# Key norms and values by one-pass transposes, sums and centring on VectorE, and a new order of the planned region

## The chip, the cores and the metric

The kernel runs on one core of a Trainium2 chip. Its five engines work side by side: TensorE (PE in the profile; PEld is its weight loads), VectorE (DVE), ScalarE (ACT), GpSimd (POOL) and SyncE (SP, which here only issues DMAs). The metric is the time of one execution in microseconds of the device. Three runs of the kernel before took 892.96, 894.33 and 895.68 us, so the median is 894.33 us. One further execution was profiled; it took 893.92 us, and its trace spans 891.5 us from the first instruction to the last.

## The reference, cut to what matters

One decoder layer on 16 meta tokens and 512 tokens of width 1024, in float32: a sliding-window attention and an RWKV-7 time mixing with 16 heads of 64, merged by gates, then an output projection, a layer norm and an MLP. The change touches the time mixing alone:

```python
kk = kh * k_k.astype(f32).reshape(H, N)
kk = kk / jnp.maximum(jnp.sqrt(jnp.sum(kk * kk, -1, keepdims=True)), 1e-12)
...
def step(S, inp):
    r_t, w_t, k_t, v_t, kk_t, a_t = inp
    sa = jnp.einsum('bhij,bhj->bhi', S, -kk_t)
    S = S * w_t[:, :, None, :] + sa[..., None] * (kk_t * a_t)[:, :, None, :] + v_t[..., None] * k_t[:, :, None, :]
    return S, jnp.einsum('bhij,bhj->bhi', S, r_t)
...
ym = jnp.mean(y, -1, keepdims=True)
yv = jnp.mean(jnp.square(y - ym), -1, keepdims=True)
y = ((y - ym) * lax.rsqrt(yv + GN_EPS)).reshape(B, T, W) * lnx_g.astype(f32) + lnx_b.astype(f32)
```

For each head and token this needs the sum of 64 squared keys (the key norm), and it takes the mean of 64 outputs away from each output before the variance. The output is linear in v, so a v whose mean over the 64 channels of a head has been taken away gives outputs whose mean is already away.

## The kernel before, in words

The program has two parts. The first, up to about 560 us of the trace, is a region planned by hand: the functions `lead`, `head`, `rwkv`, `attention`, `merge`, `merged`, `out_half` and `first_norm` do not emit instructions but record 3087 operations, each with an engine, the buffers that it reads and writes, and a closure that emits it. `Plan.order` then emits them in the order of the list `ORDER`; `SLOTS` says for each new buffer which slot of its ring it gets (eight PSUM banks in the ring `rg`, and rings in SBUF). Each engine takes its instructions in that order, and waits where an input or a slot is not free yet. The second part, the MLP, is written in order behind the region and is not touched.

The time mixing and the attention work on pairs of heads: `rwkv(j)` and `attention(j)` for j from 0 to 7, with 128 channels (two heads of 64) on the partitions and 528 tokens along the row. Dense products (`dense`, eight input blocks of 128, two at a time) split every float32 weight and input in two parts of a shorter float type and take three products (lines 454 to 456 of the profile); ACT makes the one part of the weights (line 611) and DVE the other (line 613). They stand between the many small steps of the pairs in the order, and are what PE does while a pair waits.

A product of plain float32 operands stands in the trace as two records, a transpose (`pe.transpose`, a product with the identity) as one. The steps that the change touches are, in each pair:

- **Key norms**, `norms`, lines 987 to 989. `sq` holds the squared scaled keys, channels on partitions. Five float32 products with `ones2`, a constant of two columns that has a one where a channel belongs to a head, give the two sums per token, tokens on partitions, in ten columns of the bank `mt`. A sixth product for the meta tokens (line 989) goes to the same bank. DVE clamps the ten columns (line 992) and takes the reciprocal (line 994), and POOL spreads the result to `dv`, `dvm` and `dvx` (lines 999 to 1008), by which scores are scaled (line 1039) on the way to the triangular solve of the pair, a long row of small steps on POOL (lines 1122 and 1126).
- **Values**, `turn_v`, line 1096, and `meta0`, lines 1194 and 1195. Four float32 products of v with `center` (the identity less 1/64 within a head) turn v to tokens on partitions and centre it at the same time; a fifth does so for the meta tokens.
- **The state and the outputs**. `link` (line 1243) carries the state from one chunk of 64 tokens to the next, with a scaling on DVE (line 1225) and on ACT (line 1228) between two links; `outs` (line 1253) gives the outputs in the bank `Y`.
- **Group norm of the outputs**, lines 1264 to 1277: ACT squares `Y` into `ysq`, DVE sums each 64 (line 1265) and scales the sums (line 1266), POOL takes the power -1/2 (line 1267), DVE multiplies `Y` by it into `yn` (line 1268), PE turns it back by transposes (`turn_y`, line 1273), ACT applies gain and bias (line 1276) and POOL adds the bonus (line 1277). The last pair does this in two halves, since the output projection (lines 1418 to 1420) and the first norm (line 1482 and on) wait for it.

Of the kernel before, what the change touches and what calls it, by code (L numbers as in the profile page):

```python
# [14 lines left out]
AF = mybir.ActivationFunctionType  # L15
# [61 lines left out]
for _name, _c in ROWS:  # L77
# [304 lines left out]
def hybrid_layer_kernel(ctx: ExitStack, tc: tile.TileContext, I: dict, out: bass.AP):  # L382
# [26 lines left out]
    def cv(name):  # L409
        a, w = CONSTS[name]  # L410
        return con[:, a : a + w]
# [1621 lines left out]
```

## Time and profile before

| | |
|---|---|
| runs | 892.96, 894.33, 895.68 us; median 894.33 us |
| the profiled execution's own time | 893.92 us |
| its span | 891.5 us, granted TensorE clock 0.996 |
| ACT busy | 518.1 us (58%) |
| POOL busy | 286.3 us (32%) |
| DMA | 115.85 MB, mean 130 GB/s |

A line of a busy table gives the busy time of an engine and its share of the span, then the number of its instructions. In the line by slices each digit is the busy share, in tenths, of a fortieth of the span (22.3 us). A group of instructions reads: line, engine, operation, what it writes and reads with shapes, the count, busy time in us, mean duration in ns, and the idle time of the engine just ahead of it with what ended it. A line of a timeline reads: start in us, duration in us, engine, line, operation. The duration of a product on PE is from its start until its last result is out, and the next one starts long before that; what a product takes of PE's time is the distance from its start to the next start. ACT and DVE also do the splitting of the weights for PE, and POOL the triangular solves; the DMA queues load weights all through the span.

### The profile page before, as it was taken

The page shows a single profiled execution, that of the slowest core. Times are in us where ns is not written, and L with a number is a line of the kernel's source. Part 1 is how long each engine was busy: PE and PEld are TensorE (multiplying, and loading weights), DVE is VectorE, ACT ScalarE, POOL GpSimd, SP SyncE. Part 2 cuts the span into 40 slices and gives each one's busy share as a digit, 9 for nine tenths or more (in the row PEclk, how much of TensorE's full clock was granted, in tenths as well). Part 3 has the DMA queues.
Part 4 walks back from the last instruction along what each step waited for, and adds up shares of the span by engine and source line. Part 5 has one row for each costly group of instructions (what it writes and reads, how often), then busy time and mean ns, then how long its engine had stood idle before and what let it go on. Part 6 is the DMA issues. An engine that isn't in the chain of part 4 may idle for free.

```text
span 891.5 us, 17504 instructions
## 1 busy us (share of the span) xinstructions
PE 873.5 (98%) x6712; PEld 764.2 (86%) x6712; DVE 675.8 (76%) x1192; ACT 518.1 (58%) x1131; POOL 286.3 (32%) x672
## 2 busy tenths in 40 slices
PE   7999999999999999999999999999999999999996
PEld 7899989898898988887878777988888888888885
DVE  7665876878778678568588789597877886788757
ACT  8645658546585584563855545755555655564700
POOL 4038265275472751832836602000010000000001
PEclk9999999999999999999999999999999999999999
DMA  7233324322524323232345631485687578576222
GB/s 267 88 102 106 101 90 112 83 67 57 153 72 113 123 67 94 67 101 62 117 104 167 193 107 53 123 280 147 165 214 205 149 209 245 142 201 165 99 92 94
DMA packets 73531, 115.85 MB, mean 130 GB/s; under 512 B 40310, under 2 KB 47736, under 8 KB 69480
## 3 DMA queue, kind: packets, MB, share of 16 engines
q1 hardware_dynamic: 69728, 98.89, 35.6%
q0 software_dynamic: 2880, 14.68, 9.1%
q8 instruction: 52, 0.85, 0.4%
q10 hardware_dynamic: 840, 1.17, 0.4%
q14 instruction: 31, 0.25, 0.1%
HBM read 107.56 MB, written 8.21 MB: 130 GB/s over the span
## 4 chain that ended last, share of the span: by engine, by line
PE 80%; POOL 6%; DVE 6%; issue 4%; ACT 2%; DMA 1%; SPq 0%; DVEq 0%; POOLq 0%; ACTq 0%
PE g L454 9%; PE g L455 9%; PE g L456 9%; PE dnR L1798 7%; PE rq L1704 5%; PE tp L1704 4%; PE dnP L1798 4%; PE last L1798 4%; PE dnT L1798 3%; PE up L455 3%; PE up L454 3%; PE up L456 3%; POOL Xf L1126 2%; POOL ftmp L1122 2%; PE g L1182 2%
## 5 line engine op out<-in xcount | busy, mean ns | idle before, releaser
L454 PE MATMUL g<-hhi,whi 128*128 128x512 f32 (+3 forms) x640 | 211.9, 331 | 0.4 <-ACT whi L611 0.4
L455 PE MATMUL g<-hlo,whi 128*128 128x512 f32 (+3 forms) x640 | 203.6, 318 | 0.1
L456 PE MATMUL g<-hhi,wlo 128*128 128x512 f32 (+3 forms) x640 | 203.4, 318 | 0.2 <-DVE wlo L613 0.2
L454 PEld LDWEIGHTS g<-hhi,whi 128*128 128x128 f32 x640 | 120.8, 189 | 11.3 <-issue 1.4
L1122 POOL TENSOR_TENSOR ftmp<-Xf,Nf 108x84 f32<-108x84 f32 (+23 forms) x248 | 95.9, 387 | 104.2 <-DMA Nf<-Nd 75.3
L456 PEld LDWEIGHTS g<-hhi,wlo 128*128 128x128 f32 x640 | 120.6, 188 | 9.1 <-DVE wlo L613 0.8
L455 PEld LDWEIGHTS g<-hlo,whi 128*128 128x128 f32 x640 | 120.9, 189 | 7.6 <-DVE hlo L817 0.3
L613 DVE TENSOR_TENSOR wlo<-wraw,whi 128x512 fp32r<-128x512 f32 x126 | 89.7, 723 | 27.3 <-ACT whi L611 20.6
L1126 POOL TENSOR_TENSOR Xf<-Xf,ftmp 108x84 f32<-108x84 f32 (+23 forms) x248 | 104.2, 420 | 18.4
L611 ACT CAST whi<-wraw 128x512 fp32r<-128x512 f32 x126 | 76.6, 619 | 33.7 <-DMA wraw<-in_w_in_dram 15.9
L1788 POOL DMA_DIRECT2D braw<-in_w_ff_dram x12 | 10.7, 890 | 204.4 <-DVE wlo L1605 87.8
L1228 ACT ACTIVATE Z<-g,PC 64x64 f32<-64x64 f32 x64 | 19.7, 309 | 77.5 <-DVE Z L1225 39.9
L1605 DVE TENSOR_TENSOR wlo<-wraw,whi 128x1024 fp32r<-128x1024 f32 x22 | 26.9, 1222 | 12.8 <-ACT whi L1601 12.8
L1225 DVE TENSOR_SCALAR Z<-g,PC 64x64 f32<-64x64 f32 x64 | 17.5, 274 | 25.0 <-PE g L1243 11.9
L1267 POOL TENSOR_TENSOR rs<-rs,mhalf 128x8 f32<-128x8 f32 (+1 forms) x9 | 15.9, 1764 | 60.9 <-DVE rs L1266 60.8
L1601 ACT CAST whi<-wraw 128x1024 fp32r<-128x1024 f32 x22 | 22.9, 1042 | 18.2 <-PE dnR L1798 5.8
L1605 DVE TENSOR_TENSOR blo<-braw,bhi 128x1024 fp32r<-128x1024 f32 x25 | 30.5, 1219 | 2.4 <-ACT bhi L1601 2.4
L1605 DVE TENSOR_TENSOR wlo<-braw,whi 128x1024 fp32r<-128x1024 f32 x25 | 30.5, 1219 | 2.4 <-ACT whi L1601 2.4
L1601 ACT CAST whi<-braw 128x1024 fp32r<-128x1024 f32 x25 | 26.3, 1052 | 5.1 <-PE rq L1704 4.3
L1601 ACT CAST bhi<-braw 128x1024 fp32r<-128x1024 f32 x25 | 26.3, 1051 | 3.5 <-DMA braw<-in_w_ff_dram 3.5
L454 PE MATMUL up<-h1hi,whi 128*128 128x512 f32 x72 | 28.1, 390 | 0.0
L455 PE MATMUL up<-h1lo,whi 128*128 128x512 f32 x72 | 28.1, 390 | 0.0
(532 smaller groups left out, 2455.1 us busy)
## 6 DMA issues: line engine op xcount, KB each, us to landing
wraw<-in_w_in_dram SPq DMA_DIRECT2D x52, 512.0 KB
braw<-in_w_ff_dram SPq DMA_DIRECT2D x19, 1024.0 KB
wraw<-in_w_ff_dram SPq DMA_DIRECT2D x32, 512.0 KB
braw<-in_w_ff_dram POOLq DMA_DIRECT2D x12, 1024.0 KB, 8.3
wraw<-in_w_out_dram SPq DMA_DIRECT2D x14, 256.0 KB
Nf<-Nd SPq DMA_DIRECT2D x24, 144.0 KB
res<-in_x_dram SPq DMA_DIRECT2D x4, 512.0 KB
G<-in_consts_dram SPq DMA_DIRECT2D x16, 128.0 KB
```

The costliest lines, as they stand in the source:

```text
L454: pe.matmul(ps, whi, xhi, start=first, stop=False)
L455: pe.matmul(ps, whi, xlo, start=False, stop=False)
L456: pe.matmul(ps, wlo, xhi, start=False, stop=last)
L611: AC(512, lambda hi=hi, qs=qs: act.copy(hi.t, raw.t[:, qs]), plain=True, r=[raw], w=[hi], new=[hi])
L613: f = lambda hi=hi, lo=lo, qs=qs, e=e: e.tensor_tensor(lo.t, raw.t[:, qs], hi.t.bitcast(F32), op=ALU.subtract)
L1122: sub(nj * nt, lambda s=s, nj=nj, nt=nt, tv=tv: pool.tensor_tensor(tv(), Xf.t[:, 0:nj, s : s + 1].to_broadcast([NB, nj, nt]), Nf.t[:, s : ...
L1126: sub(nj * nt, lambda s=s, nj=nj, tv=tv: pool.tensor_tensor(Xf.t[:, 0:nj, s + 1 :], Xf.t[:, 0:nj, s + 1 :], tv(), op=ALU.add), port=1, r=[ ...
L1228: op("ACT", 335, lambda: act.activation(Z.t[H2[1], c, 1, :], src(1), AF.Copy, scale=PC.t[H2[1], last : last + 1]), r=[ps, PC], w=[(Z, ("s" ...
L1601: act.copy(like(s["r"][0][:, :n], s["x"]), s["x"])
L1605: dve.tensor_tensor(lo, s["x"], hi.bitcast(F32), op=ALU.subtract)
L1704: pe.matmul(o, l[:, ks], r[:, k], start=start and k == c == 0, stop=stop and k == 3 and c == 2, skip_group_check=True)
L1798: pe.matmul(acc[b], l[:, as_], r[:, ws], start=first and i == 0 and q == 0, stop=last and i == NP - 1 and q == 2, skip_group_check=True)
```

## The change

Three products become transposes, and VectorE does what the constants did. The operation counts of the other engines stay.

- `norms`: five transposes of `sq`, four into a bank of its own, `kt_`, and one into columns 128 to 255 of `mt`, and the product for the meta tokens as before. DVE sums each 64 of the four (one `tensor_reduce` over 512 columns) and then, in one operation `inverse`, each 64 of the meta tokens' 128 columns, the clamp and the reciprocal.
- `turn_v` and the second product of `meta0`: transposes with the identity, so v is not centred any more.
- The outputs: DVE sums each 64 of `Y` into the new `ym` and writes `yn` = `Y` - `ym`/64 (a `scalar_tensor_tensor`), ACT squares `yn` in place of `Y`, and the last multiplication works on `yn` in place.
- The constants `center` and `ones2` are gone, 130 columns of the table of constants.
- `ORDER` has 3105 operations (two more for each of nine output parts) and is another order throughout; `SLOTS` is written anew with it. The costs in the code say what the planner counts with: 1300 becomes 760 for `norms`, 896 becomes 442 for `turn_v`, 335 becomes 225 for `meta0`.

```diff
-    out["center"] = np.eye(P) - bones / HD
-    out["ones2"] = (p[:, None] // HD) == np.arange(2)[None, :]
...
+    rym = ring("ym", rb, [P, 8], 2)
...
-        mt, d1, dv, dvm = Buf(rg), Buf(rd1), new("dv", rdv), Buf(rdvm)
+        mt, kt_, d1, dv, dvm = Buf(rg), Buf(rg), Buf(rd1), new("dv", rdv), Buf(rdvm)
...
-                pe.matmul(mt.t[:, 2 * i : 2 * i + 2], sq.t[:, t0 : t0 + P], cv("ones2"), start=True, stop=True)
-            pe.matmul(mt.t[:, 8:10], sq.t[:, 0:P], cv("ones2"), start=True, stop=True)
+                pe.transpose(kt_.t[:, i * P : (i + 1) * P], sq.t[:, t0 : t0 + P], ident)
+            pe.transpose(mt.t[:, P : 2 * P], sq.t[:, 0:P], ident)
...
-        op("PE", 1300, norms, r=[sq, BKm, AXm], w=[(mt, "s")], new=[mt], mode="F")
-        op("DVE", 80, lambda: dve.tensor_scalar(d1.t, mt.t[:, 0:10], 1e-24, None, op0=ALU.max), r=[(mt, "s")], w=[d1], new=[d1])
-        op("DVE", 120, lambda: dve.reciprocal(d1.t, d1.t), r=[d1], w=[d1])
+        op("PE", 760, norms, r=[sq, BKm, AXm], w=[(mt, "s"), kt_], new=[mt, kt_], mode="F")
+        DV(512, lambda: dve.tensor_reduce(d1.t[:, 0:8], kt_.t.rearrange("p (u i) -> p u i", i=HD), axis=AX.X, op=ALU.add), r=[kt_], w=[d1], new=[d1])
+        def inverse():
+            dve.tensor_reduce(d1.t[:, 8:10], mt.t[:, P : 2 * P].rearrange("p (u i) -> p u i", i=HD), axis=AX.X, op=ALU.add)
+            dve.tensor_scalar(d1.t, d1.t, 1e-24, None, op0=ALU.max)
+            dve.reciprocal(d1.t, d1.t)
+        op("DVE", 400, inverse, r=[(mt, "s"), d1], w=[d1])
...
-                pe.matmul(vt.t[:, i * P : (i + 1) * P], v.t[:, t0 : t0 + P], cv("center"), start=True, stop=True)
-        op("PE", 896, turn_v, r=[v], w=[vt], new=[vt, Z], mode="F")
+                pe.transpose(vt.t[:, i * P : (i + 1) * P], v.t[:, t0 : t0 + P], ident)
+        op("PE", 442, turn_v, r=[v], w=[vt], new=[vt, Z], mode="T")
...
-            pe.matmul(ms.t[:, 0:P], v.t[:, 0:P], cv("center"), start=True, stop=True)
+            pe.transpose(ms.t[:, 0:P], v.t[:, 0:P], ident)
...
-            AC(n, lambda cs=cs: act.activation(ysq.t[:, cs], Y.t[:, cs], AF.Square), r=[(Y, k) for k in yk(j, h)], w=[(ysq, h)], new=[ysq] if one else [])
+            DV(n, lambda us=us, u8=u8: dve.tensor_reduce(ym.t[:, us], u8(Y.t), axis=AX.X, op=ALU.add), r=[(Y, k) for k in yk(j, h)], w=[(ym, h)], new=[ym] if one else [])
+            DV(n, lambda us=us, u8=u8: dve.scalar_tensor_tensor(u8(yn.t), B64(ym.t[:, us], HD), -1.0 / HD, u8(Y.t), op0=ALU.mult, op1=ALU.add),
+               r=[(ym, h)] + [(Y, k) for k in yk(j, h)], w=[(yn, h)], new=[yn] if one else [])
+            AC(n, lambda cs=cs: act.activation(ysq.t[:, cs], yn.t[:, cs], AF.Square), r=[(yn, h)], w=[(ysq, h)], new=[ysq] if one else [])
...
-            DV(n, lambda us=us, u8=u8: dve.tensor_tensor(u8(yn.t), u8(Y.t), B64(rs.t[:, us], HD), op=ALU.mult),
-               r=[(rs, h)] + [(Y, k) for k in yk(j, h)], w=[(yn, h)], new=[yn] if one else [])
+            DV(n, lambda us=us, u8=u8: dve.tensor_tensor(u8(yn.t), u8(yn.t), B64(rs.t[:, us], HD), op=ALU.mult),
+               port=1, r=[(rs, h)], w=[(yn, h)])
```

The rest of the diff is the two lists, `ORDER` and `SLOTS`.

More of the change, by code (lines that the diff above doesn't have):

```diff
@@ L1194, in meta0 @@
             pe.transpose(ms.t[0:48, 320:448], BKm.t, ident)
-            pe.matmul(ms.t[:, 0:P], v.t[:, 0:P], cv("center"), start=True, stop=True)
-        op("PE", 335, meta0, r=[BKm, v, XTm, AKm], w=[(ms, 0), (ms, "b")], new=[ms, BTm, SVm, RHm], mode="F")
+            pe.transpose(ms.t[:, 0:P], v.t[:, 0:P], ident)
+        op("PE", 225, meta0, r=[BKm, v, XTm, AKm], w=[(ms, 0), (ms, "b")], new=[ms, BTm, SVm, RHm], mode="F")
         DV(128, lambda: dve.tensor_tensor(BTm.t, ms.t[0:48, 320:448].rearrange("p (h j) -> p h j", h=2), B64(dvm.t, HD), op=ALU.mult),
@@ L1257, in rwkv @@
                w=[(Y, h)], new=[Y] if h == 0 else [], mode="C")
-        ysq, yn, rs = Buf(re_), Buf(re_), Buf(rrs)
+        ysq, yn, rs, ym = Buf(re_), Buf(re_), Buf(rrs), Buf(rym)
         yt, z = Buf(rg), new("z", rz)
```

323 rows, old and new, of tables (ORDER, SLOTS) are left out of this document.

## The prediction

> **What bounds the kernel now.** I read the page first, for which engine has no room, then the waits of PE, then busy time by stretch, and last the timeline of PE at the steps that change.
>
> ```profile
> span 891.5 us, 17504 instructions
> ...
> PE 873.5 (98%) x6712; PEld 764.2 (86%) x6712; DVE 675.8 (76%) x1192; ACT 518.1 (58%) x1131; POOL 286.3 (32%) x672
> ```
>
> PE is idle for 18.0 us of 891.5. The waits of PE, by what ended them, are 13 rows that sum to 9.6 us; the first three and the last:
>
> ```profile
> PE g L688 <- DMA con<-in_consts_dram: 3.2, 1, 3.2
> PE g L799 <- DVE res L766: 1.5, 1, 1.5
> PE g L1243 <- ACT Z L1228: 1.2, 3, 0.7
> ...
> PE g L456 <- DVE wlo L613: 0.2, 1, 0.2
> ```
>
> The first two belong to the start, ahead of any pair; no other row is over 1.2 us. So the planned region is a stream of products, and what PE no longer has to issue there shortens it, unless something else comes late in its place. How much room the other engines have shows in busy time by stretch (columns: stretch, its length, then PE, PEld, DVE, ACT, POOL, the granted clock, DMA share, GB/s): the whole region, and two stretches in which DVE is fullest.
>
> ```profile
> 0.00:560.00 560.00, 549.80 (x4918) 480.95 (x4919) 422.12 (x881) 342.79 (x878) 263.66 (x647) 1.00 0.37 106
> 320.00:360.00 40.00, 40.00 (x428) 34.95 (x428) 34.57 (x72) 23.43 (x58) 9.90 (x22) 1.00 0.29 76
> 520.00:560.00 40.00, 39.05 (x314) 31.18 (x314) 36.54 (x76) 22.75 (x56) 6.41 (x7) 1.00 0.22 67
> ```
>
> DVE, to which the change adds, is idle for 560 - 422.1 = 137.9 us of the region, but only for 5.4 us of the 40 from 320 and 3.5 us of the 40 from 520.
>
> **What PE saves.** A busy time overlaps the next product, so I take a block's cost from its first start to the first start behind it. The timeline of PE, at four places:
>
> ```profile
> 65.86 0.60 PE L1084 MATMUL g<-con,BK 128*128 128x128 f32 x4
> 66.21 0.37 PE L454 MATMUL g<-hhi,whi 128*128 128x264 f32 x1
> ...
> 102.32 0.27 PE L1194 MATMUL g<-con,BKm 128*48 128x128 f32 x1
> 102.43 0.39 PE L1195 MATMUL g<-con,e 128*128 128x128 f32 x2
> 102.57 0.37 PE L454 MATMUL g<-hhi,whi 128*128 128x264 f32 x1
> ...
> 153.26 1.05 PE L1096 MATMUL g<-con,res 128*128 128x128 f32 x8
> 154.07 0.48 PE L454 MATMUL g<-hhi,whi 128*128 128x512 f32 x1
> 154.39 0.40 PE L455 MATMUL g<-hlo,whi 128*128 128x512 f32 x1
> 154.63 0.39 PE L456 MATMUL g<-hhi,wlo 128*128 128x512 f32 x1
> ...
> 158.33 0.95 PE L987 MATMUL g<-con,res 128*128 128x2 f32 x8
> 159.14 0.36 PE L988 MATMUL g<-con,res 128*128 128x2 f32 x2
> 159.44 0.28 PE L989 MATMUL g<-AXm,BKm 128*48 128x32 f32 x2
> ```
>
> Four transposes that exist already (line 1084) take 66.21 - 65.86 = 0.35 us, one record each. A transpose with another product of this kind behind it takes 102.43 - 102.32 = 0.11 us.
>
> - Values: eight records take 154.07 - 153.26 = 0.81 us; four transposes will take 0.35. Saved: 0.46 us a pair.
> - Key norms: ten records take 159.44 - 158.33 = 1.11 us, though they stream two columns each: the 128-column weight load sets their pace. Five transposes at 0.11 us take 0.55. Saved: 0.56 us.
> - Meta values: two records take 102.57 - 102.43 = 0.14 us; the one transpose is the fifth of a group of transposes, (0.35 - 3 x 0.11) = 0.02 us up to a dense product. Saved: 0.12 us at most, 0.03 if it takes a full 0.11.
>
> Together 1.14 us a pair, less the last doubt 1.05; over eight pairs 8.4 to 9.1 us. I take 9.0.
>
> Here the Trainium skill says otherwise. "TensorE: Matmul & The Clock Gate", Part 4 (PE-mode transpose), gives about 275 ns for a transpose in one kernel's context, and says that transposes do not count as PE being busy for the clock gate. By it ten transposes a pair would cost 2.75 us. The trace agrees with that figure as a duration and not as a cost: the row of line 1084 lasts 0.60 us for four, while the next product starts 0.35 us behind the first of them.
>
> **What the new order costs on PE.** The first dense product behind another kind takes longer: 154.39 - 154.07 = 0.32 us, the next one 154.63 - 154.39 = 0.24. Matching the two lists ORDER to the operations, I count 126 entries into dense runs on PE before and 140 after. 14 more at 0.08 us are 1.1 us lost.
>
> Against that stands one stretch that a new order will most likely not repeat. The granted clock, in busy time by stretch:
>
> ```profile
> 389.00:390.00 1.00, 0.76 (x6) 0.68 (x6) 1.00 (x3) 0.98 (x4) 0.00 (x0) 0.73 0.19 44
> 390.00:391.00 1.00, 1.00 (x4) 0.65 (x3) 1.00 (x2) 0.95 (x3) 0.00 (x0) 0.50 0.46 102
> 391.00:392.00 1.00, 1.00 (x4) 0.67 (x4) 0.95 (x3) 1.00 (x4) 0.00 (x0) 0.50 0.89 201
> 392.00:394.00 2.00, 2.00 (x12) 1.76 (x11) 1.96 (x3) 1.87 (x5) 0.00 (x0) 0.78 0.75 289
> ```
>
> PE ran at half its clock for some 3.4 us, which costs up to 0.27 + 0.50 + 0.50 + 2 x 0.22 = 1.7 us. It is the one such stretch between the start and the end, so I put it down to this order's waits around 389 us, next to the key norms of a pair. I take 1.7 us as gained, with 0 (it happens once again) and -1.7 (twice) kept in the range.
>
> **What DVE pays.** The groups of DVE whose shapes are nearest:
>
> ```profile
> L1482 DVE SCALAR_TENSOR_TENSOR res<-res,g 128x512 f32<-128x512 f32 x8 | 5.4, 680 | 0.0
> ...
> L1265 DVE TENSOR_REDUCE rs<-e 128x8 f32<-128x512 f32 x5 | 3.4, 677 | 0.0
> ...
> L992 DVE TENSOR_SCALAR d<-g 128x10 f32<-128x10 f32 x8 | 1.3, 164 | 3.1 <-PE g L989 1.7 <-POOL dvx L1008 1.3
> ...
> L1265 DVE TENSOR_REDUCE rs<-e 128x4 f32<-128x256 f32 x2 | 0.8, 420 | 0.3 <-ACT e L1264 0.2
> ```
>
> A pair gets a sum over 512 columns for the norms (0.68), one over 128 (between the 0.164 of ten columns and the 0.42 of 256; 0.29 halfway), the sum of Y (0.68) and the centring (0.68, line 1482 reads a bank in the same way): 2.33 us. The last pair has two halves, 0.42 for 0.34 each time, 0.3 us more. Clamp and reciprocal stay, and the last multiplication only moves from a bank to SBUF, which I price at nothing, since the sum over SBUF and the centring product over a bank above take the same. Over eight pairs 18.9 us, 441 of a region of about 551 us: 80% in place of 75%.
>
> What of it reaches PE has a bound on either side: 0, if the idle 137.9 us takes it all, and 18.9, if all of it stands in the way. Queued behind these operations on DVE are the second parts of the weights (line 613), the scalings between two links (line 1225) and the evictions of dense products, all of which PE waits for in the end. I take 1.0 us, near the low end, because those same things wait behind 422 us of DVE work now and all waits of PE together are 9.6 us.
>
> Two chains get longer. Norms to `dv` by a sum and the meta sum, 0.97 us, ahead of POOL's spreading and the triangular solve: hidden by the dense products, if the norms stand that much earlier in the order, and in the new ORDER they do: eight times of eight they come no later among PE's operations, or within one place (places 68, 123, 207, 275 of 746 for 70, 127, 208, 279). Outputs to `yn`, 1.4 us longer: only the last pair has a reader close behind it, and there the timeline has
>
> ```profile
> 539.27 0.69 PE L1253 MATMUL g<-Z,G 128*64 128x64 f32 x16
> ...
> 543.45 0.38 PE L1273 MATMUL g<-con,e 128*128 128x128 f32 x2
> ```
>
> 4.2 us from the last outputs to their transposes, filled with output products. With 2 x 0.42 us more the new order must leave 5.0 us; if it leaves what stood here, PE waits 0.8 us, which is inside the 1.0. A gain stands against it that I price at nothing: the bank of `Y` comes free after the centring, not after ACT, POOL and the last multiplication. The two constants that go shorten one load that nobody waits for long: nothing.
>
> **Sum**, against the profiled 893.9 us: -9.0 + 1.1 - 1.7 + 1.0 = -8.6, so 885.3 us. The median of the runs is 0.4 above the profiled execution, so I predict 885.7 us. About 0.3% (2.7 us) is what a measurement of this kernel can tell from no change.
>
> **The rivals.**
>
> - The waits of the order shrink too, below 880 us. Of the 9.6 us of waits 4.9 are behind the start, and the 8.4 us of idle time beyond the rows hold shorter ones; an order searched under drawn delays should have more slack. But the 9.6 were found for the order before, which has little left to give. Chance 0.12.
> - The saving is half eaten, 889 to 896 us: the new order was made for a mean over several delays, and gives PE 4 to 9 us of small waits where the old one had fewer. For it: two stretches with DVE at 86% and 91%. Against it: PE has dense products as filler everywhere. Chance 0.16.
> - DVE becomes the bound: slower. Place: 320 to 360 and 520 to 560 us, where 5.4 and 3.5 us of DVE are idle. Two pairs' share, 4.7 us, fits in neither twice. Price: up to 18.9 us, so at worst 893.9 - 9.0 + 18.9 = 903.8 us. It decides from the point where more than 9 us of the 18.9, a half, come through to PE; then the time is above 894. The region's 137.9 us speak against that. Chance 0.09.
> - Transposes cost their full duration on PE. From rows: ten at 0.27 us are 2.7 us a pair in place of 0.81 + 1.11 + 0.14 = 2.06, 5.1 us more in all, 899 us. The 0.35 us for four speaks against it. Chance 0.01. It is the rule of the Trainium skill named above ("TensorE: Matmul & The Clock Gate", Part 4).
> - The change doesn't do what it says: transposes of `sq` or v go as two records, since the data are float32. Then PE saves only one record of ten (0.11 us a pair at best) and the time is 893 to 895. All transposes in the trace are float32 and go as one (four rows for four). Chance 0.02.
> - The forecast, 880 to 889 us: 0.60.
>
> **How the numbers follow.** Faster by over 0.3% is below 891.6 us: the forecast, the first rival and nearly half of the second, 0.60 + 0.12 + 0.07 = 0.79. Within 0.3%: the rest of the second and the two-record case, 0.10. Slower, above 897.0: 0.11, with the ends of the second rival. The range runs from 879.5 us (the sum with 6 us of waits less) to 893 us (the sum with half of the DVE work coming through).
>
> **What would show it.** In the profile after: lines 1096 and 1195 with half the records and a block of four at 0.35 us; the norms' block at 0.55 us; PE's records down by ten a pair, 80 in all; DVE's busy time up by 18 to 20 us; the waits of PE not above 12 us; the second part of the program as long as before, about 330 us. I am wrong if PE's waits on DVE grow by more than 4 us, if PE's blocks do not shrink as said, or if the region shrinks by less than 5 us with the blocks as said.

## The result and the profile after

The changed kernel takes 885.17 us (median of 4 runs, 884.26 to 885.79) against 894.65 us (4 runs, 892.96 to 895.68) for the kernel before on the same chip: a ratio of 0.9902, 95% interval 0.9888 to 0.9915. Predicted were 885.7 us. Of all executions in this document one, of a later kernel, ran at a granted clock of 0.85 and took 952.0 us; it is left out. The profiled execution took 884.26 us, the fastest of its four; its span is 882.5 us. The page's head and its row of engines:

```profile
span 882.5 us, 17352 instructions
...
PE 863.8 (98%) x6632; PEld 751.8 (85%) x6632; DVE 691.0 (78%) x1226; ACT 516.8 (59%) x1131; POOL 291.2 (33%) x672
```

PE has 80 records fewer and DVE 34 instructions more. PE is busy for 9.7 us less than before (863.8 for 873.5) and idle for 0.7 us more (18.7 for 18.0). The changed blocks, in the timeline of PE (start, duration):

```profile
155.37 0.60 PE L987 MATMUL g<-con,e 128*128 128x128 f32 x4
155.80 0.27 PE L988 MATMUL g<-con,e 128*128 128x128 f32 x1
156.00 0.28 PE L989 MATMUL g<-AXm,BKm 128*48 128x32 f32 x2
...
158.15 0.27 PE L1199 MATMUL g<-con,BKm 128*48 128x128 f32 x1
158.26 0.27 PE L1200 MATMUL g<-con,res 128*128 128x128 f32 x1
158.28 0.48 PE L453 MATMUL g<-sghi,gwh 128*128 128x512 f32 x1
...
181.05 0.60 PE L1101 MATMUL g<-con,e 128*128 128x128 f32 x4
181.41 0.48 PE L1022 MATMUL g<-rk,bones 128*128 128x512 f32 x1
```

The norms take 156.00 - 155.37 = 0.63 us (1.11 before), the values 0.36 (0.81), the meta values 0.02 (0.14). The waits of PE, by what ended them, are 11 rows; the first three and the last:

```profile
PE g L688 <- DMA con<-in_consts_dram: 5.6, 1, 5.6
PE g L1151 <- DVE U L1158: 0.9, 2, 0.7
PE g L1508 <- DVE res L1502: 0.9, 2, 0.6
...
PE g L1214 <- DMA XTm<-xtd: 0.2, 1, 0.2
```

The first row is new in size: 5.6 us for the first constant, where it was 3.2. Behind it no row is over 0.9 us, and the rows sum to 4.9 us (6.4 before). Busy time by stretch (columns as before) for the region, the two stretches in which DVE was fullest, and the second of these 9 us earlier:

```profile
0.00:560.00 560.00, 548.94 (x4910) 477.08 (x4911) 442.50 (x925) 348.75 (x894) 269.49 (x648) 1.00 0.38 109
320.00:360.00 40.00, 40.00 (x433) 34.61 (x432) 32.76 (x71) 21.00 (x57) 14.83 (x41) 1.00 0.34 102
520.00:560.00 40.00, 38.61 (x257) 32.28 (x258) 34.61 (x76) 25.57 (x61) 6.91 (x8) 1.00 0.29 93
511.00:551.00 40.00, 38.59 (x307) 30.44 (x304) 37.71 (x80) 20.68 (x50) 5.98 (x7) 1.00 0.22 65
```

Up to 560 us DVE is 20 us busier, but the region ends earlier now: up to its end, at 565 and at 574 us, it is 15.2 us (443.9 for 428.8). In the first of the two stretches where I had put a rival DVE is less busy than before. The work of the second now stands some 9 us earlier, and there DVE is fuller: 37.7 us of 40, where it was 36.5. The first product of the second part, in the timelines of before and after, says where the 9 us went:

```profile
574.12 0.40 PE L454 MATMUL up<-h1hi,whi 128*128 128x512 f32 x1
```
```profile
565.11 0.40 PE L453 MATMUL up<-h1hi,whi 128*128 128x512 f32 x1
```

The region ends 9.0 us earlier; what follows takes 891.5 - 574.1 = 882.5 - 565.1 = 317.4 us in both.

### The profile page after: what moved, and what is told of

Same layout as the page of the kernel before. It is cut to its first block, busy times and chain, and to the rows that moved or that the text cites. A ratio compares the mean times of both kernels' runs of the same rounds, so it can differ in the third digit from the quotient of the medians.

```text
span 882.5 us, 17352 instructions
## 1 busy us (share of the span) xinstructions
PE 863.8 (98%) x6632; PEld 751.8 (85%) x6632; DVE 691.0 (78%) x1226; ACT 516.8 (59%) x1131; POOL 291.2 (33%) x672
## 4 chain that ended last, share of the span: by engine, by line
PE 88%; DVE 6%; ACT 2%; DMA 2%; issue 1%; SPq 0%; POOL 0%; DVEq 0%; ACTq 0%
PE g L453 11%; PE g L454 11%; PE g L455 11%; PE dnR L1806 7%; PE rq L1712 5%; PE tp L1712 4%; PE dnP L1806 4%; PE last L1806 4%; PE dnT L1806 3%; PE up L453 3%; PE up L454 3%; PE up L455 3%; PE g L1248 2%; PE g L1187 2%; PE g L1305 2%; PE g L1374 1%
## 5 line engine op out<-in xcount | busy, mean ns | idle before, releaser
L453 PE MATMUL g<-hhi,whi 128*128 128x264 f32 (+3 forms) x640 | 212.4, 332 | 0.0
L454 PE MATMUL g<-hlo,whi 128*128 128x264 f32 (+3 forms) x640 | 203.3, 318 | 0.5 <-DVE hlo L817 0.4
L455 PE MATMUL g<-hhi,wlo 128*128 128x264 f32 (+3 forms) x640 | 202.9, 317 | 0.0
L1127 POOL TENSOR_TENSOR ftmp<-Xf,Nf 108x84 f32<-108x84 f32 (+23 forms) x248 | 98.6, 398 | 110.4 <-DMA Nf<-Nd 58.0
L613 DVE TENSOR_TENSOR wlo<-wraw,whi 128x512 fp32r<-128x512 f32 x126 | 87.7, 705 | 25.7 <-ACT whi L611 21.4
L1131 POOL TENSOR_TENSOR Xf<-Xf,ftmp 108x84 f32<-108x84 f32 (+23 forms) x248 | 101.1, 408 | 18.5
```

The lines of the kernel that those rows point to most:

```text
L453: pe.matmul(ps, whi, xhi, start=first, stop=False)
L454: pe.matmul(ps, whi, xlo, start=False, stop=False)
L455: pe.matmul(ps, wlo, xhi, start=False, stop=last)
L613: f = lambda hi=hi, lo=lo, qs=qs, e=e: e.tensor_tensor(lo.t, raw.t[:, qs], hi.t.bitcast(F32), op=ALU.subtract)
L1127: sub(nj * nt, lambda s=s, nj=nj, nt=nt, tv=tv: pool.tensor_tensor(tv(), Xf.t[:, 0:nj, s : s + 1].to_broadcast([NB, nj, nt]), Nf.t[:, s : ...
L1131: sub(nj * nt, lambda s=s, nj=nj, tv=tv: pool.tensor_tensor(Xf.t[:, 0:nj, s + 1 :], Xf.t[:, 0:nj, s + 1 :], tv(), op=ALU.add), port=1, r=[ ...
```

## The experiments

All ratios are to the kernel before on the same chip, with 95% intervals. The experiments ran in three groups on different chips, so times of different groups are compared through these ratios. "Against the changed kernel" is the difference of two such ratios (0.9902 for the changed kernel) times 893.9 us; its own uncertainty is about 1.6 us, from the two intervals.

**PE's blocks put back, everything else left.** The new order and VectorE's work stay, and the ten transposes of a pair become products with the identity, so two records again:

```diff
-                pe.transpose(kt_.t[:, i * P : (i + 1) * P], sq.t[:, t0 : t0 + P], ident)
+                pe.matmul(kt_.t[:, i * P : (i + 1) * P], sq.t[:, t0 : t0 + P], ident, start=True, stop=True)
...
-                pe.transpose(vt.t[:, i * P : (i + 1) * P], v.t[:, t0 : t0 + P], ident)
+                pe.matmul(vt.t[:, i * P : (i + 1) * P], v.t[:, t0 : t0 + P], ident, start=True, stop=True)
```

In full (P stands for PE's blocks as the source of the gain, O for the order):

> The changed kernel with its own order and its VectorE work, but all ten transposes a pair (norms, values, meta values) written as plain products with the identity, which take two records each on PE. Theory P (the gain is what PE no longer issues, the new order gives nothing net): values 0.81 for 0.36 us, norms 1.11 for 0.64, meta 0.14 for 0.03, 1.03 us a pair, 8.2 us in all: 893.4 us, ratio to before about 0.999. Rival O (the gain is the new order's shorter waits, and PE's own saving hides behind waits): less than 3 us come back, under 888 us, ratio under 0.993.

The norms alone (D: VectorE or waits besides):

> The changed kernel with the five transposes of the key norms alone written as products with the identity (two records each). Theory P: 1.11 for 0.64 us a pair, 3.8 us in all, 889.0 us. Rival O: within 1.5 us of the changed kernel. A third theory D (the norms sit ahead of a chain that decides: sum, reciprocal, spreading, triangular solve) expects more than PE's own 3.8 us, 6 us or more.

The values and meta values alone:

> The changed kernel with the values' and meta values' transposes alone written as products with the identity. Theory P: (0.81 - 0.36) + (0.14 - 0.03) = 0.56 us a pair, 4.5 us in all, 889.7 us, and the parts of this run and of the one with the norms add up to the run with both. Rival O: within 1.5 us of the changed kernel.

Measured: in full 891.24 us, ratio 0.9973 (0.9962 to 0.9984), so 6.3 us above the changed kernel; norms alone 891.16, 0.9970 (0.9958 to 0.9982), 6.1 us; values alone 888.34, 0.9941 (0.9929 to 0.9953), 3.5 us. Summed over PE's timeline, start to next start, the three blocks of all pairs take 9.2 us more in the first than in the changed kernel (18.2 for 9.0), so by the medians some two thirds of what PE saves there reaches the end. The two traces alone say more: their spans differ by 7.8 us (890.3 and 882.5), PE's busy time by 8.0, and PE is idle for about as long (18.5 and 18.7 us). The parts do not add: 6.1 + 3.5 is 9.6, and both together are 6.3 (by the spans of the traces 6.4 + 2.5 = 8.9, and 7.8).

The norms put back add 4.6 us to their own blocks (9.7 for 5.1), which is inside the uncertainty of the 6.1. In their trace PE is idle for 2.2 us more than in the changed kernel (20.9 us); the rows that grew most are the transposes of the outputs (line 1281, 1.4 us) and line 1214 behind a DMA (1.1 for 0.2).

With the old cost on PE and the new work on VectorE, the kernel is still 2.4 us (1.4 to 3.4) faster than before: that is the order's.

**Two ways to take VectorE's price.** Each added DVE instruction issued twice, order and PE as changed:

```diff
-        DV(512, lambda: dve.tensor_reduce(d1.t[:, 0:8], kt_.t.rearrange("p (u i) -> p u i", i=HD), axis=AX.X, op=ALU.add), r=[kt_], w=[d1], new=[d1])
+        f = lambda: dve.tensor_reduce(d1.t[:, 0:8], kt_.t.rearrange("p (u i) -> p u i", i=HD), axis=AX.X, op=ALU.add)
+        DV(512, lambda f=f: [f(), f()], r=[kt_], w=[d1], new=[d1])
```

> The changed kernel in its own order with every new VectorE instruction issued twice (both sums, the meta sum, the centring), 19 us more of VectorE, no other difference. Theory P (VectorE has room): 1 to 2 us more, 886 to 887 us. Rival D (it is close to the bound): 890 us or more.

and, later, the sums cut short:

```diff
-            DV(n, lambda us=us, u8=u8: dve.tensor_reduce(ym.t[:, us], u8(Y.t), axis=AX.X, op=ALU.add), ...
+            DV(n, lambda us=us, u8=u8: dve.tensor_reduce(ym.t[:, us], u8(Y.t)[:, :, 0:8], axis=AX.X, op=ALU.add), ...
```

> The changed kernel, with every added sum of VectorE read over 8 of 64 columns (the rest of each sum is left out; the norm is scaled by 64 instead), so about 10 us less on VectorE and everything else as it was. If half of every us on VectorE reaches the end, on this side as on that of the doubled additions, about 880 us. If the searched order covers what is there and only more comes through (a knee at the changed kernel), at least 884.

The shortened sums leave out 56 of 64 columns, so that kernel does not compute the layer; it serves for its time alone. The doubled kernel takes 894.22 us, ratio 1.0009 (1.0000 to 1.0018); the shortened one 884.67, 0.9891 (0.9875 to 0.9908). The row of engines of both, doubled first:

```profile
PE 867.2 (97%) x6632; PEld 752.5 (84%) x6632; DVE 707.7 (79%) x1260; ACT 516.1 (58%) x1131; POOL 290.9 (33%) x672
```
```profile
PE 864.2 (98%) x6632; PEld 752.4 (85%) x6632; DVE 682.4 (77%) x1226; ACT 516.8 (59%) x1131; POOL 292.2 (33%) x672
```

8.6 us less on DVE (691.0 - 682.4) is worth 1.0 us, not to be told from nothing; 16.7 us more (707.7 - 691.0) costs 9.6 us. So the price is not the same on both sides: 0.12 us per us of DVE below (give or take 0.22), 0.57 above. The 8.6 us that were taken away from VectorE are nearly covered, and of the next load more than half comes through; where between the three points the bend lies is not shown, and the doubled instructions also lengthen the chains in which they stand. Of the 9.1 us between the spans of the doubled and the changed kernel 5.7 are idle time of PE. Its waits show it in many small rows that the changed kernel does not have:

```profile
PE g L1076 <- DVE res L1382: 1.4, 1, 1.4
PE g L987 <- DVE res L1273: 1.0, 1, 1.0
PE g L1378 <- DVE pown L1371: 1.0, 1, 1.0
...
PE g L1091 <- DVE e L1392: 0.9, 1, 0.9
PE g L1038 <- DVE e L656: 0.8, 1, 0.8
```

Only line 987 waits for a doubled instruction (the centring, line 1273 there); the others wait for DVE work that shares DVE's queue with the doubled ones: the multiplications of the gates (lines 1382 and 1392), attention's mask (line 1371), evictions of dense products (line 656).

**The change in the order of before.** The old list ORDER, with the new operations put in at the old places of their kind: the sum and the centring right ahead of the squares, the sums of the norms right behind the norms. Free buffers were given out anew.

> The change in the order of the kernel before: the old ORDER, each new sum and centring put right ahead of its square, each sum of squared keys right behind its norms (eight PSUM banks do not hold one more there for long), slots as before where they are free. PE's blocks fall from 9.1 + 7.5 + 1.9 to 5.1 + 2.9 + 1.0 us, 9.5 us. Theory P (the gain is what PE no longer issues, whatever the order, and VectorE's 19 us hide): 885 to 887 us. Rival O (a new order was needed to find room for VectorE's work): 889 us or more. If it is 883 or less, the new order is worse than the old one for this work.

The same with the transposes as two records:

> As the run in the old order, but with the transposes written as products with the identity: PE issues what it did before (ten products of two records a pair), so this is VectorE's added work alone in the old order. Theory P: 0.5 us more on PE, VectorE hides: 894 to 896 us. Rival D (VectorE's 19 us reach PE): 898 us or more.

and a second try, with the norms' sums at the clamp's old place where eight banks allow it:

> The change in the old ORDER again, with the sums of the norms where the clamp stood (two of eight directly behind the norms) and the banks of the sums chosen for the widest gap to their next user. If the old order has no room for the 19 us that VectorE gets (the new order is what makes room), at least 900 us, a few us better than the 913.8 of the first try. If the first try's loss came from where I had put sums and banks, under 893.

Measured: 913.81 us, 1.0222 (1.0204 to 1.0240); 913.92, 1.0228 (1.0211 to 1.0244); 909.87, 1.0181 (1.0162 to 1.0200). In the old order PE's 9 us are worth nothing that can be told from noise (first and second differ by 0.5 us, give or take 2.2; in their traces the first has PE 7.1 us less busy and 6.5 us more idle). VectorE's work, with the places and banks that it got here, costs 16 to 20 us. The waits of PE in the second try, the first five rows:

```profile
PE g L1362 <- DVE d L992: 4.6, 1, 4.6
PE g L688 <- DMA con<-in_consts_dram: 3.2, 1, 3.2
PE g L1210 <- ACT SVm L1205: 1.8, 2, 1.4
PE g L455 <- DVE wlo L613: 1.6, 3, 1.2
PE g L1248 <- ACT Z L1233: 1.6, 3, 0.7
```

The first is of my making: attention's turned weights got the bank in which a norms' sum was late. If all its 4.6 us went, the kernel would still be some 11 us slower than before. Among the other rows are two that I had named: the second parts of the weights (line 613), and the scalings of the links, here on ACT's side (line 1233). In all PE is idle for 35.2 us (18.0 before). A third cost is the clock, in busy time by stretch (the granted clock is third from the end):

```profile
165.00:169.00 4.00, 4.00 (x72) 3.59 (x70) 2.54 (x8) 1.97 (x7) 2.72 (x9) 0.57 0.04 6
400.00:404.00 4.00, 3.83 (x14) 3.30 (x15) 3.91 (x7) 3.48 (x10) 0.00 (x0) 0.60 0.67 202
462.00:469.00 7.00, 4.09 (x12) 3.42 (x13) 4.69 (x10) 1.93 (x4) 2.10 (x12) 0.52 0.39 68
```

Three stretches at half clock, where the trace of the kernel before has one. An order searched for the new work but with the old one as its start was not tried, so these times are no bound on what a better placing by hand could reach.

**The start.** The new order issues the first 512 KB of x on SyncE's queue ahead of the meta tokens; the old one the other way round. SyncE's rows in the timelines of before and after:

```profile
0.74 0.39 SPq L693 DMA_DIRECT2D sb<-in_meta_dram  x1
1.19 2.04 SPq L682 DMA_DIRECT2D res<-in_x_dram  x4
```
```profile
0.75 0.39 SPq L682 DMA_DIRECT2D res<-in_x_dram  x1
1.20 0.41 SPq L693 DMA_DIRECT2D sb<-in_meta_dram  x1
```

The constant that PE's first product waits for is loaded from ACT's queue, and nothing of it changed. Tested from both sides, by exchanging these loads in the head of ORDER (and the slots of what they load):

```diff
-    0, 127, 6, 7, 2, 128, 1, 26, 67, 5, 41, ...
+    0, 127, 6, 7, 26, 2, 128, 1, 67, 5, 41, ...
```

for the changed kernel (S: the start's loads), and the reverse in the kernel before:

> The changed kernel with one step of the order moved: the load of the meta tokens is issued ahead of the first 512 KB of x, as in the kernel before. In the changed kernel PE's first product starts at 5.56 us of the span, before at 3.24, and everything up to the first dense product is 2.2 us later. Theory S (x's load ahead of the small loads delays the identity that PE waits for, and the delay runs on to the end): PE starts at about 3.3 us, and the time falls by 2 us to about 883.2. Rival C (the late start is chance, or is taken up by a wait further on): no change within 0.7 us.

> The kernel before with the first 512 KB of x issued ahead of the load of the meta tokens, as in the changed kernel. Theory S: PE's first product moves from 3.2 to about 5.5 us, and the time grows by 1 to 2 us, to 895 or 896. Rival C: no change within 0.7 us.

The changed kernel with the meta tokens first takes 884.01 us, 0.9890 (0.9878 to 0.9903); the kernel before with x first takes 895.77, 1.0025 (1.0015 to 1.0034). The wait of PE for the first constant, in the one and in the other:

```profile
PE g L688 <- DMA con<-in_consts_dram: 3.3, 1, 3.3
```
```profile
PE g L688 <- DMA con<-in_consts_dram: 5.4, 1, 5.4
```

So the order of two loads on another queue moves this constant by 2.2 to 2.3 us. In the kernel before it costs 2.2 us of the time (1.3 to 3.0), in the changed one about 1.1, inside the uncertainty. With the meta tokens first the changed kernel has the lowest ratio of all that were run, but not clear of its own without.

**Each part alone, in the new order.** Norms by transposes and sums, with the values centred on PE again and no sum or centring on VectorE (the multiplication reads the bank of `Y`, as before; some 45 buffers got other slots), and the reverse:

```diff
-                pe.transpose(vt.t[:, i * P : (i + 1) * P], v.t[:, t0 : t0 + P], ident)
+                pe.matmul(vt.t[:, i * P : (i + 1) * P], v.t[:, t0 : t0 + P], cv("center"), start=True, stop=True)
```

> The new order with the first part of the change alone: norms by transposes and sums, values centred on TensorE again, without the sums and centring on VectorE (12 us less there) but with the values' and meta values' records doubled (plus 5.4 us of PE's blocks, of which 3.4 reached the end when they were put back alone). If VectorE's time reaches the end by half: 885.2 + 3.4 - 6 = 882.6 us. If VectorE's additions are covered in this order: 888.6.

```diff
-                pe.transpose(kt_.t[:, i * P : (i + 1) * P], sq.t[:, t0 : t0 + P], ident)
+                pe.matmul(mt.t[:, 2 * i : 2 * i + 2], sq.t[:, t0 : t0 + P], cv("ones2"), start=True, stop=True)
```

> The new order with the second part alone: values by transposes and centring on VectorE, norms by products with the two columns again (4.0 us more in PE's blocks, 6.9 us less on VectorE). If PE's blocks come through and VectorE is covered: 889 us. If VectorE's time comes through by half as well: 886. If longer norm blocks cost more than their own time (putting back the records alone cost 6.0): 889 to 891.

The norms' part alone takes 891.82 us, 0.9981 (0.9970 to 0.9992); the values' part alone 887.27, 0.9923 (0.9907 to 0.9938). The second lies between the 886 us of VectorE's time coming through by half and the 889 of the other readings, and its uncertainty against the changed kernel, 1.8 us, decides for neither. The first fits neither of mine: 10.9 us less on DVE (680.1 busy), and 3.6 us *slower* than the kernel that has the same PE blocks with all of VectorE's work (values put back alone, 888.34). Its waits of PE show one reason, in a row that the changed kernel does not have:

```profile
PE g L1088 <- DVE e L1272: 1.3, 1, 1.3
```

Line 1272 is there the multiplication that reads `Y`'s bank, and by the lists of that kernel one pair's transposes of line 1088 get this bank two places behind it in ORDER. The bank comes free only behind ACT's square, POOL's power and DVE's multiplication, where the change frees it behind the centring. This is 1.3 of the 3.6 us; what makes the rest is not shown, since so many slots differ too.

## Why the prediction was right

The time came within 0.5 us of the forecast. That it came so near is partly luck. On PE's side the sum was right: -9.0 + 1.1 - 1.7 = -9.6 us were forecast, and in the traces PE's busy time fell by 9.7. Its idle time was to grow by 1.0 and grew by 0.7, but by two changes that nearly cancel and that the sum did not have: 2.4 us more for the first constant, and 1.7 us less behind it. The experiments, with their wider errors, move the shares further: less of PE's saving and more of the order. Step by step:

- **PE's blocks** shrank as said: start to next start, summed over PE's timeline, norms 9.1 to 5.1 us, values 7.5 to 2.9, meta values 1.9 to 1.0, in all 9.5 for the 9.0 of the sum. Two errors stand against each other in it: the norms' block takes 0.64 us a pair and not 0.55, since the last transpose has a product of another kind behind it (156.00 - 155.80 = 0.20 us), and the values took 0.94 before on the average of the pairs, not the 0.81 of the place that I read. The transposes cost their distance, not their 0.27 us; the Trainium skill's 275 ns ("TensorE: Matmul & The Clock Gate", Part 4) is again the duration in the rows (0.27 us), as the page has it too, and not what PE pays. The weak step is the next one, silently taken: that all of it reaches the end. Of 9.2 us, 6.3 (give or take 1.6) did by the medians, and 7.8 by the two traces.
- **The order on PE** was priced at +1.1 - 1.7. The 1.1 stands: up to the second part PE's timeline has 13 more first products of dense runs (lines 454 to 456 before; 120 for 107), each some 0.32 us for the 0.23 of a next one. With PE's old cost and VectorE's new work in it the kernel is 2.4 us faster than before, and that holds the late start (1.1 to 2.2 us) and VectorE's share (about 1) against it. So by these numbers, each with an uncertainty of 1 to 2 us, the order is worth some 4 to 6 us by itself, not 0.6. The traces of that kernel and of the one before show 3.3 us of it: PE's busy time is 1.7 us shorter, about the half clock of the sum, and its idle time behind the first constant 1.6 (13.2 for 14.8). The first rival's mechanism, shrinking waits, was at work inside the forecast. The groups of the links, before and after, show it best, with their idle time in the last column:

```profile
L1243 PE MATMUL g<-Z,G 128*128 128x128 f32 x112 | 23.2, 289 | 1.4 <-ACT Z L1228 1.2
```
```profile
L1248 PE MATMUL g<-Z,G 128*128 128x128 f32 x112 | 22.8, 285 | 0.2
```

- The **half clock** did go, in the one trace that each kernel has: the stretch 300 to 400 us of before has 0.98 and that of after 1.00.

```profile
300.00:400.00 100.00, 99.39 (x917) 86.74 (x917) 72.94 (x155) 63.74 (x169) 48.80 (x121) 0.98 0.30 84
```
```profile
300.00:400.00 100.00, 99.35 (x986) 86.75 (x985) 78.45 (x167) 66.52 (x174) 46.45 (x117) 1.00 0.33 92
```

- **VectorE** at +1.0: the size is not contradicted (8.6 us of the 18.9 are worth 1.0 +- 1.9; the other 10 were not taken away by themselves). The reason that I gave, that what PE waits for stands behind 422 us of DVE work anyway, does not hold: the same work in the old order, as it was placed there, costs 16 to 20 us. In the new order it is covered. Busy time rose by 15.2 us, not 18.9, with the added instructions as priced; line 613's group, for one, shrank from 89.7 to 87.7 us.
- **The rival that DVE becomes the bound** did not come, though its second place got fuller, not emptier: of 40 us there DVE is idle for 2.3, and PE for 1.4 (3.5 and 0.9 before). It is not far off: of the further 16.7 us of the doubled kernel more than a half comes through, the share that I had put as its point for the first 18.9.
- **The start** was missing. Of a moved step every DMA counts, and I had not compared the heads of the two lists: 2.4 us later on PE, 1.1 to 2.2 us of time.
- **The last pair**: I asked for 5.0 us between the last outputs and their transposes. The timeline of PE after, and the one row on these transposes in the waits of the kernel with all blocks put back:

```profile
527.99 0.69 PE L1258 MATMUL g<-Z,G 128*64 128x64 f32 x16
...
533.07 0.44 PE L1281 MATMUL g<-con,e 128*128 128x128 f32 x2
```
```profile
PE g L1281 <- DVE e L1276: 1.1, 1, 1.1
```

  The new order leaves 5.1 us, and the waits after have no row for line 1281. Where PE's steps are longer, the same order makes PE wait there: one of the ways in which the parts do not add.
- **Two slips** that do not move the forecast: the second part takes 317.4 us, not about 330, because the region ended at 574 us and not at 560; and the upper end of the range, half of VectorE's work coming through, is 885.7 - 1.0 + 9.4 = 894.1, not 893.

What stays open: how much of PE's saving is lost (1.3 to 4.5 us by the medians, 1.4 by the traces) and through which waits, since the rows of the two traces show none. All tests of single parts were made in orders fitted to other durations, so each also measures that misfit.

## What to carry to other kernels

Where one engine is full, moving work from it to another with a quarter of its time idle paid here in the order made for it and not in the old one, as I placed it there: measure the same edit in the old order, too, before crediting the edit or the order. Double the added work once and halve it once; the two slopes tell whether what you have is still covered. And compare the first loads of two orders: a load on one queue can hold back a constant on another.

## What the runs showed of the hardware

With a load of 512 KB issued at 0.75 us in place of 1.19 on SyncE's queue, ahead of the 64 KB of the meta tokens and not behind them, a 64 KB load that ACT's queue issues at 0.74 us releases PE 2.2 to 2.3 us later (5.4 for 3.2 and 5.6 for 3.3 us, two pairs of kernels).

The half-clock stretch stands at nearly the same place in two traces of the old order. With only the first loads exchanged it comes again in the kernel before, some 3.4 us later; busy time by stretch of that kernel:

```profile
393.00:394.00 1.00, 1.00 (x3) 0.81 (x4) 0.99 (x2) 1.00 (x4) 0.00 (x0) 0.50 0.98 228
394.00:395.00 1.00, 1.00 (x4) 0.81 (x4) 0.96 (x3) 0.98 (x3) 0.00 (x0) 0.50 0.89 342
```

The old order with VectorE's new work has two or three such stretches in its traces, and the kernels in the new order none ahead of their last microseconds. Each kernel has one trace, so how much of this is chance is not shown. Executions of one kernel do differ: of 51 executions of the kernel before, 25 had a mean granted clock of 0.996 (893.7 us on average), 12 had 0.998 (892.6 us) and four 0.992 (896.5 us). A mean does not tell where in the span the clock fell. What in the order brings the stretch on was not tested.
